# A hybrid decoder trunk on one Trainium2 core: four seven-product pairs in place of three in gate/up groups 1, 4 and 8, and a hold around the first such pair's load

## The chip, the cores and the metric

The program runs on one core of one Trainium2 chip. The core has five engines with an instruction queue each: TensorE (PE, matrix products; its weight loads are listed as PEld), VectorE (DVE), ScalarE (ACT), GpSimd (POOL) and SyncE (SP, which issues the transfers). An engine runs its instructions in the order in which the program holds them. Tiles lie in SBUF; matmul results accumulate in PSUM banks of 128 x 512 float32.

The metric is the device time of one execution in microseconds, the median of several runs. Beside it there is one profiled execution with its trace.

## The reference

Two decoder layers (DEPTH 2) over a residual stream of 256 tokens (SEQ) and 2048 features (D_MODEL), all in float32. The mixers (sliding-window attention with an mLSTM in layer 0, forgetting attention in layer 1) are not touched by the change. What is touched is the feed-forward part, with FFN_HIDDEN = 5632:

```python
def rms_norm(x, g):
    xf = x.astype(jnp.float32)
    y = xf * lax.rsqrt(jnp.mean(xf * xf, axis=-1, keepdims=True) + RMS_EPS)
    return (y * g.astype(jnp.float32)).astype(x.dtype)
...
def swiglu(xn, w_gate, w_up, w_down):
    return (jax.nn.silu(xn @ w_gate) * (xn @ w_up)) @ w_down
...
    for layer in range(DEPTH):
...
        h = h + mix.astype(h.dtype)
        h = h + swiglu(rms_norm(h, norm_ffn[layer]), w_gate[layer], w_up[layer], w_down[layer])
    return rms_norm(h, norm_final)
```

## The kernel before

**Precision.** TensorE multiplies in the format fp32r. To keep float32 accuracy every operand is split into a high part (ACT casts it, L206 or L379) and a low part (DVE subtracts the cast from the value, L207 or L380), and every product is three matmuls: high x high, high x low, low x high (`three`, L556 to L558). So a chunk of weights costs a load, a cast on ACT and a subtraction on DVE before PE can use it.

**Tiling.** The 256 tokens are two row blocks of 128. The contraction over 2048 features is 16 steps of 128, taken as eight pairs of steps. Gate and up are made together in eleven *groups* of 512 columns each; a group multiplies the normalised input (transposed, in `xh` and `xl`) by 512 columns of `w_gate` and 512 of `w_up`, which gives four results of 128 x 512 (two row blocks, gate and up), `acc` in the order. `ffn` runs the groups in three parts (0 to 2, 3 to 6, 7 to 10) and after each part multiplies what it made by the matching rows of `w_down`.

**Two kinds of pairs.** A pair of contraction steps is a 2 x 2 block product: two row blocks by two steps, and two steps by the columns of gate and up. A *plain* pair makes it with 8 products, 24 matmuls: per weight matrix one chunk of 128 x 1024 (`load_chunk`), split by one cast and one subtraction (L206, L207). A *seven-product* pair makes it with 7 products, 21 matmuls, after the scheme of Strassen and Winograd: it loads both chunks into one tile (`quad`), forms three differences of weights on DVE (L646, 128x2x512; L649 and L650, 128x512), and casts and splits three pieces (L379 and L380: one of 128 x 1536 into a triple, two of 128 x 1024 into slots). The matching sums of the inputs are made once per layer ahead of the groups; those for pair 7 (`FOURTH`, with the tile `x4`) are made too. Four of the seven products go into a second set of PSUM banks, `prod`; after the group's last seven-product pair `combine` makes from them one tile `c` of four results (one copy on ACT at L576, three additions on DVE at L578 to L580).

The table `ORDER` sets a group: five plain pairs and three seven-product pairs (1, 3 and 5), two plain ones last. `HEAVY` is a table with four of each, that ends with the plain pair 6. `DENSE` names the groups that use `HEAVY`; it is empty before.

**The end of a group.** Four additions at L697 put the accumulators and `c` together, which also frees their PSUM banks; ACT applies silu; two scaled products at L701 finish; the result goes through two transposing transfers and a `join` that splits it for the down projection. The two sets of PSUM banks change places from group to group (`par`): the `prod` banks of a group are the banks of the previous group's accumulators, so a group's first product waits for an addition at L697.

**Buffers.** Split chunks live in five slots of a high and a low tile (`hi_…`), seven-product pairs in two triples (`hi0_…`/`hi1_…` of 128 x 1536) and three quads; `c` has one buffer.

**What sets the order.** The code is not run in the order in which it is written: a scheduler estimates a timeline for all engines and puts the instructions of each engine in the order of that timeline. So another table of pairs moves instructions on all engines. `tc.issue_after(x)` is a way to hold back what is issued inside its block until x has been placed.

Of the kernel before, what the change touches and what calls it, by code (L numbers as in the profile page):

```python
# [1 line left out]

# [21 lines left out]
NB = 512  # L24
CK = 2
# [10 lines left out]
ORDER = ((0, 0), (1, 1), (0, 2), (1, 3), (0, 4), (1, 5), (0, 6), (0, 7))  # L36
HEAVY = ((1, 1), (0, 0), (1, 3), (0, 2), (1, 5), (0, 4), (1, 7), (0, 6))
FOURTH = 7
DENSE = ()
DOWN = {  # L40
    6: ((0, 0), (1, 1), (0, 2), (1, 3), (0, 4), (0, 5)),
    8: ((0, 0), (1, 1), (0, 2), (1, 3), (0, 4), (1, 5), (0, 6), (0, 7)),
# [33 lines left out]
def trunk(  # L76
# [19 lines left out]
    nc = tc.nc  # L96
# [40 lines left out]
    def load_raw(w, k0, c0, n, pool=wr, bufs=4, raws=None, into=None):  # L137
        if into is not None:
            raw = into
        elif raws:  # L140
            raw = raws.pop(0)
            raws.append(raw)
        else:
            raw = pool.tile([P, CK, NB], F32, tag="raw", name="raw", bufs=bufs)
        loaded[0] = nc.sync.dma_start(
            raw[:, :, 0:n], w[k0 * P : (k0 + CK) * P, c0 : c0 + n].rearrange("(k p) n -> p k n", p=P)
        )
        return raw
# [13 lines left out]
    first = wr.tile([P, CK, NB], F32, tag="raw", name="raw", bufs=4)  # L162
# [96 lines left out]

    sums = {}  # L260

    def square_sum(key, n):
        if n == 0:
            sums[key] = sm.tile([P, NT, 4], F32, tag="ss", name="ss")
        for t in range(NT):
            junk = junk_of[0].tile([P, NB], BF16, tag=junk_of[1], name="junk", bufs=junk_of[2])
            nc.scalar.activation(
                junk, h[:, t, n * NB : (n + 1) * NB], AF.Square, accum_out=sums[key][:, t, n : n + 1]
            )

# [286 lines left out]
        nc.tensor.matmul(o, ah, lo, start=False, stop=False)  # L557
        nc.tensor.matmul(o, al, hi, start=False, stop=stop)  # L558

    def pair_group(fp, par, lhs, sums, mats, order, todo=(), halves=None, inner=None, raws=None):  # L560
        plain = [two_banks(par, "acc") for _ in range(2)]
        begun = set()

# [5 lines left out]
        todo = list(todo)  # L569
# [23 lines left out]
        for pos, (kind, pair) in enumerate(order):  # L593
            k0 = 2 * pair
# [21 lines left out]
            first, last = 1 not in kinds[:pos], 1 not in kinds[pos + 1 :]  # L616
# [5 lines left out]
            if halves:  # L622
                ra, rb = (load_raw(w, k0, c0, NB, fp, W_RAWS, raws) for w, c0 in mats)
                hg, lg = split_chunk(ra, NB)
                run_due(todo, pos)
                hu, lu = (m[:, 0, :] for m in slot())
                split_plain(hu, lu, rb[:, 0, :])
                nc.vector.tensor_tensor(out=ra[:, 1, :], in0=rb[:, 1, :], in1=ra[:, 1, :], op=ALU.subtract)
                nc.vector.tensor_tensor(out=rb[:, 1, :], in0=rb[:, 1, :], in1=rb[:, 0, :], op=ALU.subtract)
                nc.vector.tensor_tensor(out=rb[:, 0, :], in0=rb[:, 0, :], in1=ra[:, 1, :], op=ALU.subtract)  # L630
                nc.vector.tensor_tensor(out=ra[:, 0, :], in0=ra[:, 0, :], in1=rb[:, 0, :], op=ALU.subtract)
                parts = []
                for src in (ra, rb):
                    hs, ls = halves.pop(0)
                    halves.append((hs, ls))
                    split_plain(hs, ls, src)
                    parts += [(hs[:, b, :], ls[:, b, :]) for b in range(CK)]
            else:
                raw = quad()
                for m, (w, c0) in enumerate(mats):  # L640
                    load_raw(w, k0, c0, NB, into=raw[:, CK * m : CK * (m + 1), :])
                hg, lg = triple()
                latest[0] = split_plain(hg, lg, raw[:, 0:3, :])
                hu, lu = hg[:, 2, :], lg[:, 2, :]
                run_due(todo, pos)
                nc.vector.tensor_tensor(  # L646
                    out=raw[:, 1:4:2, :], in0=raw[:, 3:4, :].broadcast_to([P, 2, NB]), in1=raw[:, 1:3, :], op=ALU.subtract
                )
                nc.vector.tensor_tensor(out=raw[:, 2, :], in0=raw[:, 2, :], in1=raw[:, 1, :], op=ALU.subtract)  # L649
                nc.vector.tensor_tensor(out=raw[:, 0, :], in0=raw[:, 0, :], in1=raw[:, 2, :], op=ALU.subtract)  # L650
                (h1, l1), (h0, l0) = slot(), slot()
                split_plain(h1, l1, raw[:, 1:4:2, :])
                split_plain(h0, l0, raw[:, 0:3:2, :])
                parts = [((h0, h1)[b % 2][:, b // 2, :], (l0, l1)[b % 2][:, b // 2, :]) for b in range(4)]
# [14 lines left out]
    def ffn(layer, fp, sx, x4, sd, key, todo, idx_next=None, key_next=None, finish=None):  # L669
# [8 lines left out]
        for g0, g1 in zip(PARTS, PARTS[1:]):  # L678
            end = g1 == PARTS[-1]
            nk = 4 * (g1 - g0)  # L680
            order = DOWN[nk // 2]
            for g in range(g0, g1):
                par = (g1 - 1 - g) % 2
# [5 lines left out]
                    [(w_gate[layer], g * NB), (w_up[layer], g * NB)],  # L689
                    HEAVY if g in DENSE else ORDER,  # L690
                    todo,
                )
                todo = []
                for m in range(2):
# [59 lines left out]
                todo = [(MID if g < g1 - 1 else MID_DOWN, join)]  # L754
# [20 lines left out]
            for n0 in (0, 2):  # L775
# [9 lines left out]
                todo = []  # L785
# [50 lines left out]
    with tc.tile_pool(name="ev", bufs=1) as ev:  # L836
# [225 lines left out]
        with tc.tile_pool(name="mp", bufs=1) as mp:  # L1062
            def sums_m(pair):
# [3 lines left out]
            raws = [  # L1067
                ev.tile([P, CK, NB], F32, tag=tag, name=f"hr{a}", bufs=1 + a // 2)
                for a, tag in enumerate(("kd", "qn", "alibi", "alibi"))
            ]  # L1070
            halves = spare_halves()
# [30 lines left out]
            todo = [(AHEAD_M[m], turn(src, dst)) for m, (src, dst) in enumerate(((qm, qmt), (km, kmt)))]  # L1102
# [92 lines left out]
    with tc.tile_pool(name="od", bufs=1) as od:  # L1195
# [70 lines left out]
        halves = spare_halves()  # L1266
# [152 lines left out]
```

## Time and profile before

| what | value |
|---|---|
| median of 3 runs | 2082.78 us (2081.64 to 2082.93) |
| profiled execution, its own time | 2082.55 us |
| span of its trace | 2080.8 us |
| ACT busy | 1368.0 us |
| POOL busy | 43.2 us |
| 16 DMA engines, mean | 209 GB/s |
| loads of gate and of up | 176 each, 512.0 KB each |

The span runs from the first to the last instruction in the trace. Busy times are per engine; a matmul's shown duration of 0.39 us overlaps the next one, so a stretch of matmuls is measured from start to start. In the trace's rows the columns are the start in us from the span's beginning, the duration in us, the engine, the line, the operation with what it writes and reads (buffer numbers left out) and its size; a bracket behind a row gives the wait ahead of it and what ended it. A row "x2" stands for two instructions on end.

### The profile page before, as it was taken

How to read it: one execution, taken by the hardware profiler on the slowest of the kernel's cores; microseconds unless marked ns; L12 is line 12 of the kernel's file. 1: busy time of each engine (PE TensorE's matmuls, PEld its weight loads, DVE VectorE, ACT ScalarE, POOL GpSimd, SP SyncE). 2: the span in 40 equal slices, each digit the busy share in tenths (PEclk: the TensorE clock that was granted, in tenths of full speed). 3: DMA queues.
4: the chain of work that ended last, by engine and by line, in shares of the span. 5: the costliest groups of instructions: out<-in, count | busy, mean ns of one | idle time of the engine just before them, and what ended most of it. 6: DMA issues, size and time to landing. Idle time of an engine off the chain costs nothing.

```text
span 2080.8 us, 26492 instructions
## 1 busy us (share of the span) xinstructions
PE 2068.0 (99%) x9473; PEld 1715.3 (82%) x9473; DVE 1806.2 (87%) x2169; ACT 1368.0 (66%) x1649; POOL 43.2 (2%) x69
## 2 busy tenths in 40 slices
PE   9999999999999999999999999999999999999998
PEld 8878878888888888888888888887888888888887
DVE  6788768999899989998899688679989999989984
ACT  6777677764576656667676676587655677556763
POOL 1010000000000000000000001000000000000000
PEclk9999999999999999999999999999999999999999
DMA  8566577666676657675676776586756666666754
GB/s 295 175 206 198 188 232 232 225 209 201 191 240 219 205 192 231 210 216 174 201 220 202 227 199 185 182 253 204 229 191 203 224 197 227 219 207 196 238 156 159
DMA packets 309572, 434.84 MB, mean 209 GB/s; under 512 B 106412, under 2 KB 114624, under 8 KB 309312
## 3 DMA queue, kind: packets, MB, share of 16 engines
q1 hardware_dynamic: 307088, 426.27, 65.2%
q0 software_dynamic: 1632, 5.80, 0.9%
q8 instruction: 74, 1.21, 0.2%
q10 hardware_dynamic: 720, 1.09, 0.1%
q14 instruction: 58, 0.48, 0.1%
HBM read 408.68 MB, written 2.12 MB: 197 GB/s over the span
## 4 chain that ended last, share of the span: by engine, by line
PE 87%; DVE 5%; ACT 3%; DMA 2%; issue 2%; SPq 0%; POOL 0%; POOLq 0%; ACTq 0%; DVEq 0%
PE acc L557 20%; PE acc L558 20%; PE acc L556 20%; PE prod L556 5%; PE prod L557 5%; PE prod L558 5%; PE acc L245 4%; PE acc L244 4%; PE acc L246 4%; DVE hi L207 2%; ACT box L345 1%; DMA raw<-in_w_up_dram 1%; PE p L410 1%; DMA raw<-in_w_gate_dram 1%; DMA raw<-in_w_out_even_dram 1%
## 5 line engine op out<-in xcount | busy, mean ns | idle before, releaser
L206 ACT CAST hi<-raw 128x1024 fp32r<-128x1024 f32 (+3 forms) x561 | 567.7, 1023 | 336.9 <-PE acc L558 176.2
L207 DVE TENSOR_TENSOR hi<-raw,hi 128x1024 fp32r<-128x1024 f32 (+3 forms) x561 | 659.8, 1188 | 115.7 <-ACT hi L206 113.8
L558 PE MATMUL acc<-hi,xl 128*128 128x512 f32 x1320 | 512.2, 389 | 0.0
L379 ACT CAST hi<-raw 128x1024 fp32r<-128x1024 f32 (+2 forms) x299 | 345.8, 1169 | 247.3 <-PE acc L558 195.2
L556 PE MATMUL acc<-hi,xh 128*128 128x512 f32 x1320 | 493.6, 390 | 0.1
L557 PE MATMUL acc<-hi,xh 128*128 128x512 f32 x1254 | 488.4, 390 | 1.3 <-DVE hi L207 1.3
L556 PEld LDWEIGHTS acc<-hi,xh 128*128 128x128 f32 x1320 | 247.7, 188 | 51.7 <-ACT hi L206 0.6
L558 PEld LDWEIGHTS acc<-hi,xl 128*128 128x128 f32 x1320 | 247.8, 188 | 51.2
L557 PEld LDWEIGHTS acc<-hi,xh 128*128 128x128 f32 x1254 | 235.4, 188 | 51.9 <-DVE hi L207 2.9
L380 DVE TENSOR_TENSOR hi<-raw,hi 128x1024 fp32r<-128x1024 f32 (+1 forms) x204 | 241.1, 1183 | 18.2 <-ACT hi L379 17.8
L380 DVE TENSOR_TENSOR lo<-raw,hi 128x1536 fp32r<-128x1536 f32 x95 | 166.8, 1756 | 56.1 <-ACT hi L379 55.9
L558 PE MATMUL acc<-hi,ml 128*128 128x512 f32 x466 | 181.0, 389 | 0.0
L556 PE MATMUL acc<-hi,mh 128*128 128x512 f32 x466 | 173.2, 389 | 0.0
L557 PE MATMUL acc<-hi,mh 128*128 128x512 f32 x437 | 170.4, 390 | 0.5 <-DVE hi L207 0.5
L244 PE MATMUL acc<-hi,mh 128*128 128x512 f32 (+1 forms) x322 | 125.2, 391 | 1.4 <-DVE h L394 1.4
L245 PE MATMUL acc<-hi,mh 128*128 128x512 f32 (+1 forms) x322 | 126.3, 392 | 0.0
L246 PE MATMUL acc<-hi,ml 128*128 128x512 f32 (+1 forms) x322 | 123.9, 391 | 0.0
L646 DVE TENSOR_TENSOR raw<-raw 128x1024 f32<-128x1024 f32 x95 | 115.9, 1220 | 0.5
L556 PEld LDWEIGHTS acc<-hi,mh 128*128 128x128 f32 x466 | 87.5, 188 | 18.2
L558 PEld LDWEIGHTS acc<-hi,ml 128*128 128x128 f32 x466 | 87.5, 188 | 18.1
L245 PE MATMUL acc<-hi,xh 128*128 128x512 f32 (+3 forms) x288 | 99.8, 347 | 0.2 <-DVE hi L207 0.2
L246 PE MATMUL acc<-hi,xl 128*128 128x512 f32 (+3 forms) x288 | 99.2, 345 | 0.0
(364 smaller groups left out, 3075.0 us busy)
## 6 DMA issues: line engine op xcount, KB each, us to landing
raw<-in_w_gate_dram SPq DMA_DIRECT2D x176, 512.0 KB, 4.5
raw<-in_w_up_dram SPq DMA_DIRECT2D x176, 512.0 KB, 4.8
raw<-in_w_down_dram SPq DMA_DIRECT2D x176, 512.0 KB, 4.9
raw<-in_w_in_odd_dram SPq DMA_DIRECT2D x88, 512.0 KB, 5.1
raw<-in_w_in_even_dram SPq DMA_DIRECT2D x51, 512.0 KB, 4.8
raw<-in_w_out_even_dram SPq DMA_DIRECT2D x32, 512.0 KB, 5.1
raw<-in_w_out_odd_dram SPq DMA_DIRECT2D x32, 512.0 KB, 5.0
hr<-in_w_in_even_dram SPq DMA_DIRECT2D x12, 512.0 KB, 4.4
```

The source lines that it names most:

```text
L206: latest[0] = nc.scalar.copy(hi[:, k, 0:n], raw[:, k, 0:n])
L207: nc.vector.tensor_tensor(out=lo[:, k, 0:n], in0=raw[:, k, 0:n], in1=hi[:, k, 0:n].bitcast(F32), op=ALU.subtract)
L244: nc.tensor.matmul(o, ah[:, ts], hi, start=(k == 0), stop=False)
L245: nc.tensor.matmul(o, ah[:, ts], lo, start=False, stop=False)
L246: nc.tensor.matmul(o, al[:, ts], hi, start=False, stop=(k == k_all - 1 and cs.stop == n))
L345: nc.scalar.copy(ju[:, :, b], turned[:, b, :, :, :].rearrange("p k t q -> p (k t q)"))
L379: cast = nc.scalar.copy(dst_h, src)
L380: nc.vector.tensor_tensor(out=dst_l, in0=src, in1=dst_h.bitcast(F32), op=ALU.subtract)
L556: nc.tensor.matmul(o, ah, hi, start=start, stop=False)
L557: nc.tensor.matmul(o, ah, lo, start=False, stop=False)
L558: nc.tensor.matmul(o, al, hi, start=False, stop=stop)
L646: nc.vector.tensor_tensor(out=raw[:, 1:4:2, :], in0=raw[:, 3:4, :].broadcast_to([P, 2, NB]), in1=raw[:, 1:3, :], op=ALU.subtract)
```

## The change

It has two parts.

The first is the *hold*. `square_sum` now keeps each of its ACT instructions in a table `marks`; `pair_group` has a new argument `hold`, and group 0 of each layer passes `marks[1]`. The two loads of the group's first seven-product pair are then issued inside `tc.issue_after(hold.ins)`. That call ties only instructions of the engine on which the marked instruction runs, and that is ACT; the block holds nothing but two loads, which SP issues. The rows and the waits of all five engines with this part alone are the same as before it.

The second is `DENSE = (1, 4, 8)`: in these three groups of both layers, six groups in all, `HEAVY` sets the pairs, so that pair 7 becomes a seven-product pair and pair 6 the last, plain one; the seven-product pairs now stand first, third, fifth and seventh.

```diff
-from contextlib import ExitStack
+from contextlib import ExitStack, nullcontext
...
 ORDER = ((0, 0), (1, 1), (0, 2), (1, 3), (0, 4), (1, 5), (0, 6), (0, 7))
 HEAVY = ((1, 1), (0, 0), (1, 3), (0, 2), (1, 5), (0, 4), (1, 7), (0, 6))
 FOURTH = 7
-DENSE = ()
+DENSE = (1, 4, 8)
...
+    marks = {}
+
     def square_sum(key, n):
...
-            nc.scalar.activation(
+            marks[n] = nc.scalar.activation(
                 junk, h[:, t, n * NB : (n + 1) * NB], AF.Square, accum_out=sums[key][:, t, n : n + 1]
             )
...
-    def pair_group(fp, par, lhs, sums, mats, order, todo=(), halves=None, inner=None, raws=None):
+    def pair_group(fp, par, lhs, sums, mats, order, todo=(), halves=None, inner=None, raws=None, hold=None):
...
-                for m, (w, c0) in enumerate(mats):
-                    load_raw(w, k0, c0, NB, into=raw[:, CK * m : CK * (m + 1), :])
+                with tc.issue_after(hold.ins) if hold is not None and first else nullcontext():
+                    for m, (w, c0) in enumerate(mats):
+                        load_raw(w, k0, c0, NB, into=raw[:, CK * m : CK * (m + 1), :])
...
                     HEAVY if g in DENSE else ORDER,
                     todo,
+                    hold=marks[1] if g == 0 else None,
```

The lines behind these move by two to four: L380 becomes L382, L556 to L558 become L558 to L560, L646, L649 and L650 become L649, L652 and L653, L697 becomes L701 and L701 becomes L705. L206 and L207 stay.

In the whole program PE has 18 matmuls fewer, DVE and ACT have 24 and 6 instructions more, and the loads are as many and as large, in another order on SP's queue.

**Layer 0, from group 0 into group 1, on DVE.** Before, from the add that takes group 0's first accumulator (acc_3001 to acc_3004 are its four accumulators, c_3243 its combined tile, raw_2993 to raw_2995 the three quads, hi_2988 to hi_2992 the slots):

```order
L697 TENSOR_TENSOR c_3243<-acc_3001,c_3243 128x512
L649 TENSOR_TENSOR raw_2995<-raw_2995 128x512
L580 TENSOR_TENSOR c_3243<-prod_3038,c_3243 128x2x512
L380 TENSOR_TENSOR hi_2992<-raw_2994,hi_2992 128x1024
L207 TENSOR_TENSOR hi_2988<-raw_3400,hi_2988 128x1024
L650 TENSOR_TENSOR raw_2995<-raw_2995 128x512
L207 TENSOR_TENSOR hi_2989<-raw_3416,hi_2989 128x1024
L697 TENSOR_TENSOR c_3243<-acc_3002,c_3243 128x512
L697 TENSOR_TENSOR c_3243<-acc_3003,c_3243 128x512
L697 TENSOR_TENSOR c_3243<-acc_3004,c_3243 128x512
L380 TENSOR_TENSOR lo1_2987<-raw_2993,hi1_2986 128x1536
L701 TENSOR_SCALAR c_3243<-c_3243,r_2999 128x512
```

And the change, the twelve rows up to the chunk hi_2991<-raw_3448; between the same add at acc_3001 and these stand three more, of 128x512, 128x1024 and 128x2x512:

```order
L382 TENSOR_TENSOR hi_2990<-raw_2994,hi_2990 128x1024
L653 TENSOR_TENSOR raw_2995<-raw_2995 128x512
L382 TENSOR_TENSOR hi_2988<-raw_2995,hi_2988 128x1024
L701 TENSOR_TENSOR c_3243<-acc_3002,c_3243 128x512
L701 TENSOR_TENSOR c_3243<-acc_3003,c_3243 128x512
L701 TENSOR_TENSOR c_3243<-acc_3004,c_3243 128x512
L382 TENSOR_TENSOR lo1_2987<-raw_2993,hi1_2986 128x1536
L705 TENSOR_SCALAR c_3243<-c_3243,r_2999 128x512
L649 TENSOR_TENSOR raw_2993<-raw_2993 128x2x512
L382 TENSOR_TENSOR lo0_2985<-raw_2994,hi0_2984 128x1536
L705 TENSOR_SCALAR c_3243<-c_3243,r_2999 128x512
L207 TENSOR_TENSOR hi_2991<-raw_3448,hi_2991 128x1024
```

The adds at acc_3002 to acc_3004 have one subtraction of 1024 columns fewer ahead of them, and the stretch behind them, up to the chunk that a plain pair of group 1 waits for, now holds another subtraction of 1536 and the difference of 128x2x512 of the next seven-product pair.

**Layer 1, end of group 1 and start of group 2, on PE.** acc_11608 and acc_11609 are accumulators of group 2; hi_10974 holds the chunk raw_11612, hi_10973 the chunk raw_11680, hi0 and hi1 a seven-product pair. Before:

```order
L557 MATMUL acc_11608<-hi_10974,xh_58 128x512
L558 MATMUL acc_11608<-hi_10974,xl_59 128x512
L556 MATMUL acc_11608<-hi0_10968,xh_58 128x512
L557 MATMUL acc_11608<-lo0_10969,xh_58 128x512
L558 MATMUL acc_11608<-hi0_10968,xl_59 128x512
L556 MATMUL acc_11609<-hi_10974,xh_58 128x512
...
L556 MATMUL acc_11609<-hi_10972,xh_58 128x512
L556 MATMUL acc_11608<-hi_10973,xh_58 128x512
```

And the change:

```order
L558 MATMUL acc_11608<-hi_10974,xh_58 128x512
L559 MATMUL acc_11608<-hi_10974,xh_58 128x512
L560 MATMUL acc_11608<-hi_10974,xl_59 128x512
L558 MATMUL acc_11608<-hi1_10970,xh_58 128x512
L559 MATMUL acc_11608<-lo1_10971,xh_58 128x512
L560 MATMUL acc_11608<-hi1_10970,xl_59 128x512
L558 MATMUL acc_11608<-hi_10973,xh_58 128x512
L559 MATMUL acc_11608<-hi_10973,xh_58 128x512
L560 MATMUL acc_11608<-hi_10973,xl_59 128x512
L558 MATMUL acc_11608<-hi_10973,xh_58 128x512
```

Before, acc_11609 takes its turn at hi_10974, and hi_10973 has its first row behind that; with the change acc_11608 goes through hi_10974, the seven-product pair and hi_10973 on end, and the row that reads the low part of hi_10973 stands nine rows behind the one that reads that of hi_10974 (before, 35 rows).

**The same place on DVE.** c_11512 is group 1's combined tile, s4 and sd1 belong to the sums for the down projection, raw_10977 to raw_10979 are the quads. Before, from the one chunk to the other:

```order
L207 TENSOR_TENSOR hi_10974<-raw_11612,hi_10974 128x1024
L646 TENSOR_TENSOR raw_10979<-raw_10979 128x2x512
L578 TENSOR_TENSOR c_11512<-prod_11351,c_11512 128x512
L380 TENSOR_TENSOR sd1_10967<-s4_11525,sd0_10966 128x512
L207 TENSOR_TENSOR hi_10975<-raw_11628,hi_10975 128x1024
L649 TENSOR_TENSOR raw_10979<-raw_10979 128x512
L380 TENSOR_TENSOR hi_10976<-raw_10978,hi_10976 128x1024
L579 TENSOR_TENSOR c_11512<-prod_11350,c_11512 128x512
L697 TENSOR_TENSOR c_11512<-acc_11312,c_11512 128x512
L380 TENSOR_TENSOR hi_10972<-raw_10978,hi_10972 128x1024
L650 TENSOR_TENSOR raw_10979<-raw_10979 128x512
L207 TENSOR_TENSOR hi_10973<-raw_11680,hi_10973 128x1024
```

And the change:

```order
L207 TENSOR_TENSOR hi_10974<-raw_11612,hi_10974 128x1024
L207 TENSOR_TENSOR hi_10975<-raw_11628,hi_10975 128x1024
L653 TENSOR_TENSOR raw_10979<-raw_10979 128x512
L299 TENSOR_TENSOR s4_11520<-c_11227,s4_11520 128x128
L382 TENSOR_TENSOR lo0_10969<-raw_10977,hi0_10968 128x1536
L382 TENSOR_TENSOR hi_10976<-raw_10979,hi_10976 128x1024
L382 TENSOR_TENSOR hi_10972<-raw_10979,hi_10972 128x1024
L649 TENSOR_TENSOR raw_10977<-raw_10977 128x2x512
L207 TENSOR_TENSOR hi_10973<-raw_11680,hi_10973 128x1024
```

The combining adds, the addition at the accumulator and the subtraction for sd1 have moved ahead of the chunk raw_11612; between the two chunks there are now a split of 1536 columns and a difference of 128x2x512 in their place.

## The prediction

> **What bounds the kernel now.** I read the page first, for the engine that is never idle, then windows of the length of one gate/up group, then the timeline for the time between one instruction and the next.
>
> ```profile
> span 2080.8 us, 26492 instructions
> PE 2068.0 (99%) x9473; PEld 1715.3 (82%) x9473; DVE 1806.2 (87%) x2169; ACT 1368.0 (66%) x1649; POOL 43.2 (2%) x69
> PE 87%; DVE 5%; ACT 3%; DMA 2%; issue 2%; SPq 0%; POOL 0%; POOLq 0%; ACTq 0%; DVEq 0%
> ```
>
> PE is busy for 99% and makes 87% of the chain that ended last, so a matmul less is worth its distance to the next one. But DVE's 87% is a mean, and the change works in the gate/up groups alone. Windows of one group each (us; PE, PEld, DVE, ACT, POOL busy with counts; clock; DMA share): layer 0's groups 1, 4, 8, then layer 1's.
>
> ```profile
> 366.30:408.20 41.90, 41.77 (x184) 34.27 (x183) 41.90 (x47) 30.54 (x31) 0.00 (x0) 1.00 0.71 227
> 597.00:639.00 42.00, 42.00 (x187) 34.79 (x186) 40.95 (x46) 29.01 (x30) 0.00 (x0) 1.00 0.70 217
> 883.00:925.00 42.00, 42.00 (x187) 34.75 (x187) 39.76 (x45) 28.15 (x28) 0.00 (x0) 1.00 0.72 215
> 1427.00:1468.00 41.00, 41.00 (x183) 33.95 (x182) 40.47 (x47) 28.96 (x29) 0.00 (x0) 1.00 0.74 237
> 1657.00:1698.00 41.00, 41.00 (x183) 33.96 (x182) 39.94 (x44) 28.14 (x29) 0.00 (x0) 1.00 0.70 222
> 1943.00:1985.00 42.00, 42.00 (x187) 34.80 (x186) 39.76 (x45) 28.16 (x28) 0.00 (x0) 1.00 0.72 218
> ```
>
> In group 1 of layer 0 DVE is busy for 41.90 of 41.90 us, elsewhere for all but 0.5 to 2.2 us. There are two engines at the limit here, and the change takes work from the one and gives it to the other.
>
> **Prices.** PE first: 24 starts lie between these two.
>
> ```profile
> 704.88 0.39 PE L558 MATMUL acc<-hi,ml 128*128 128x512 f32 x1
> 710.32 0.39 PE L558 MATMUL acc<-hi,ml 128*128 128x512 f32 x1
> ```
>
> 5.44 / 24 = 0.2267 us for a matmul (its own 0.39 overlaps the next). DVE back to back, start to start:
>
> ```profile
> 399.09 1.76 DVE L380 TENSOR_TENSOR lo<-raw,hi 128x1536 fp32r<-128x1536 f32 x1
> 400.75 0.29 DVE L297 TENSOR_TENSOR s<-c,s 128x128 f32<-128x128 f32 x1
> 400.96 2.36 DVE L207 TENSOR_TENSOR hi<-raw,hi 128x1024 fp32r<-128x1024 f32 x2
> 403.23 1.22 DVE L646 TENSOR_TENSOR raw<-raw 128x1024 f32<-128x1024 f32 x1
> 404.36 0.69 DVE L578 TENSOR_TENSOR c<-prod,c 128x512 f32<-128x512 f32 x1
> 404.96 0.68 DVE L380 TENSOR_TENSOR sd<-s,sd 128x512 fp32r<-128x512 f32 x1
> 379.45 0.75 DVE L701 SCALAR_TENSOR_TENSOR c<-c,r 128x512 f32<-128x512 f32 x1
> 380.11 1.22 DVE L380 TENSOR_TENSOR hi<-raw,hi 128x1024 fp32r<-128x1024 f32 x1
> ```
>
> So 1536 columns take 1.66, 1024 take 1.135, 512 take 0.60, 128 take 0.21, and the scaled product at L701 takes 0.66.
>
> **The change, part by part.** *The held load* costs nothing: rows and waits are the same with it and without it on all five engines (the part on the change shows why), so there is nothing to hide.
>
> *PE.* A plain pair is 2 x 12 matmuls = 5.44 us, a seven-product pair 7 x 3 = 4.76 us. One pair is exchanged in each of six groups: 18 matmuls fewer, 18 x 0.2267 = **-4.1 us**, all on the path.
>
> *DVE.* A plain pair costs two subtractions of 1024, 2.27 us. A seven-product pair costs one of 1536, three of 1024 and two of 512: 1.66 + 3.40 + 1.20 = 6.27 us. The exchange adds 4.0 us to a group. An old group has 5 x 2.27 + 3 x 6.27, and about 8.6 us outside the pairs (2.34 to combine, 2.4 for four adds, 1.3 for two products, 2.5 for the join): 38.8 us against PE's 183 x 0.2267 = 41.5. A new one has 42.8 against 180 x 0.2267 = 40.8. DVE becomes the longer one by 2.0 us, and must pay from its lead, the time by which it is done before PE needs the result. That the lead, not the mean, decides is seen where the add at L697 frees the bank of a group's first product (layer 0's group 1, layer 1's group 1, layer 0's groups 4 and 8):
>
> ```profile
> 369.65 0.69 DVE L697 TENSOR_TENSOR c<-acc,c 128x512 f32<-128x512 f32 x1
> 371.77 0.39 PE L556 MATMUL prod<-hi,xh 128*128 128x512 f32 x1
> 1427.71 0.68 DVE L697 TENSOR_TENSOR c<-acc,c 128x512 f32<-128x512 f32 x1
> 1431.69 0.39 PE L556 MATMUL prod<-hi,xh 128*128 128x512 f32 x1
> 595.20 0.68 DVE L697 TENSOR_TENSOR c<-acc,c 128x512 f32<-128x512 f32 x1
> 600.84 0.39 PE L556 MATMUL prod<-hi,xh 128*128 128x512 f32 x1
> 884.83 0.69 DVE L697 TENSOR_TENSOR c<-acc,c 128x512 f32<-128x512 f32 x1
> 890.98 0.39 PE L556 MATMUL prod<-hi,xh 128*128 128x512 f32 x1
> ```
>
> The leads are 1.43, 3.30, 4.96 and 5.46 us.
>
> *Layer 0, group 1.* In the new order PE uses that bank 9 matmuls (2.04 us) earlier, DVE frees it 1.14 us earlier (a subtraction of 1024 less ahead of it): the lead there is 1.43 - 2.04 + 1.14 = 0.5 us. From there to the chunk hi_2991<-raw_3448 PE has 56 matmuls, 12.7 us, and DVE the twelve rows shown with the change and three ahead of them, 14.5 us: 0.5 + 12.7 - 14.5 = -1.3. I take **+1.3 us** of new stall. Bounds: 0, if the 1.43 us suffice; 3.3, the whole shortfall of 4.0 + 0.7 less 1.43.
>
> *Layer 1, end of group 1.* Here the new PE order has what the old one has not: it runs the first accumulator of group 2 through three pairs on end, and so asks for the chunk raw_11680 nine matmuls after raw_11612. Before, the same two uses are 7.9 us apart:
>
> ```profile
> 1459.82 2.36 DVE L207 TENSOR_TENSOR hi<-raw,hi 128x1024 fp32r<-128x1024 f32 x2
> 1467.50 0.39 PE L557 MATMUL acc<-hi,xh 128*128 128x512 f32 x1
> 1475.43 0.39 PE L557 MATMUL acc<-hi,xh 128*128 128x512 f32 x1
> ```
>
> Between the two chunks DVE has five of 1024 (the last one included), one of 1536, one of 512 and one of 128: 8.1 us; PE has nine matmuls, 2.04. The lead at the first is 5.3 us before (1467.50 less the end of the pair of subtractions that begins at 1459.82). The new order takes from it 0.7 (fewer matmuls ahead), 1.5 (DVE rows moved ahead) and 1.0 (waits that PE no longer makes, next) and leaves 2.1. So 2.1 + 2.0 - 8.1 = -4.0, **+4.0 us**. Bounds by the same rows: the lead kept whole gives 0.8, none left gives 6.1.
>
> *Waits that fall away.* Both are in layer 1's first group:
>
> ```profile
> 1414.96 0.50 PE L557 MATMUL acc<-hi,xh 128*128 128x512 f32 x1 [0.32 <-DVE hi L207]
> 1426.11 0.50 PE L557 MATMUL acc<-hi,xh 128*128 128x512 f32 x1 [0.67 <-DVE hi L207]
> ```
>
> In the new order these chunks are used some matmuls later; 0.32 + 0.67 gives **-1.0 us** (0 if they only move).
>
> *Groups 4 and 8, and the pairs behind them.* Added up row by row, the lead in the new order falls by at most some 3 to 4 us below its value at the group's start, 4.96 or 5.46, and the combining adds now wait for products that end one plain pair before the group's end, not two. What is left is between 0.8 and 2 us: no stall in the sum of rows, but little room. I take **+0.8 us** for all four groups and the way into the down projections; bounds 0 and 2.0 per group.
>
> *ACT and DMA.* ACT casts one 1536 more per new group:
>
> ```profile
> L379 ACT CAST hi<-raw 128x1536 fp32r<-128x1536 f32 x95 | 140.8, 1483 | 68.0 <-PE acc L558 31.3 <-PE prod L558 24.8 <-DMA raw<-in_w_up_dram 6.8
> raw<-in_w_gate_dram SPq DMA_DIRECT2D x176, 512.0 KB, 4.5
> ```
>
> 1.5 us on an engine that is busy for 28 to 31 of 42 us. The loads are as many and as large; on SP's queue they only change places. Both nothing, covered by ACT's idle time; if ACT's cast stood ahead of a late subtraction it would be 1.5 us a group, within the bound above.
>
> *The clock.* PE's longest pause before is 1.8 us, and it does not lower the clock:
>
> ```profile
> 278.31 0.39 PE L246 MATMUL acc<-hi,ml 128*128 128x512 f32 x1
> 280.14 0.50 PE L244 MATMUL acc<-hi,mh 128*128 128x512 f32 x1 [1.44 <-DVE h L394]
> 276.00:282.00 6.00, 4.56 (x20) 3.44 (x20) 5.50 (x6) 4.21 (x7) 0.00 (x0) 1.00 0.69 259
> ```
>
> The Trainium skill, "TensorE: Matmul & The Clock Gate" (HAM oscillation), speaks against a single long pause: an idle stretch over some 3.4 us halves TensorE's clock until it has been busy for such a stretch again. The pause that I expect in layer 1 is of that size; an estimate by that page's figure would be 1.7 us more, 2085.5 in all. No row here shows a pause so long, and I leave it out of the sum.
>
> **Sum.** -4.1 + 1.3 + 4.0 - 1.0 + 0.8 = +1.0 us. The profiled execution took 2082.55 us (span 2080.8), the median of the runs is 2082.78: 2083.6 by the one, **2083.8 us** by the other, which I predict. What PE saves, it loses again waiting for DVE. 0.2%, 4.2 us, is about what a measurement of this kernel can tell from no change.
>
> **Rivals.** (1) *Slower: DVE is the bound in every new group.* If the lead at groups 4 and 8 does not carry, each pays its 2.0 us, and the group behind, which begins with DVE late, about as much again: 4 x 2.0 to 4 x 3.5 more, so 2091 to 2097. For it: 42.8 us against 40.8, and ACT casts that DVE waits for stand in one queue with casts that wait for PE. Against: leads of 5 us, and DVE idle for 1.1 to 2.2 us in those windows. It decides once the lead at a group's start is below 3 us. (2) *Faster: the lead covers all.* Then 4.1 and the 1.0 count in full, 2077.7. For it: before, PE waits only twice for long in these groups. Against: the 8.1 us of DVE work against 2.04 of PE. (3) *The held load does hold*, and the first pair of each layer comes late or early: no row shows it; it would move one load of 4.5 us and end within 0.2%.
>
> **Numbers.** My forecast, with the cases of 2079 to 2087, 0.62; rival 1 0.26, rival 2 0.11, rival 3 0.01, which counts with the first. The sum's own bounds: all low, -4.1 + 0 + 0.8 - 1.0 = -4.3, 2078.5; all high, -4.1 + 3.3 + 6.1 + 8 = +13.3, 2096. Eight times in ten I expect 2078.5 to 2091.0: from the low bound to the first price of rival 1. Faster by over 0.2% 0.11, within 0.63, slower 0.26.
>
> **What would show it.** PE has 18 matmuls fewer at the same 0.227 us. DVE's busy time grows by some 24 us (6 x 4.0). Windows of the six groups show DVE at 100%. A PE pause of 3 to 4 us behind layer 1's group 1, released by DVE's subtraction at the line that is L207 now, and pauses of 1 to 2 us in layer 0's group 1. No pause over 1 us in groups 4, 5, 8 and 9: if there are such, rival 1 is right. If the pause in layer 1 is missing, my sum of DVE's rows is wrong there, and the time is near 2080.

## The result and the profile after

The changed kernel takes 2095.02 us (median of 6 runs, 2093.03 to 2097.52); before, 2082.93 us (6 runs, 2081.64 to 2083.21). The ratio is 1.0058, 95% interval 1.0048 to 1.0068: 12.1 us slower. The forecast was 2083.8 us and its range ended at 2091.0.

The page of the changed kernel, in the lines that answer to those shown of before:

```profile
span 2091.9 us, 26353 instructions
PE 2070.1 (99%) x9455; PEld 1710.4 (82%) x9455; DVE 1826.7 (87%) x2193; ACT 1369.7 (65%) x1655; POOL 44.2 (2%) x69
PE 75%; DVE 11%; DMA 5%; ACT 5%; issue 4%; SPq 1%; POOL 0%; ACTq 0%; POOLq 0%; DVEq 0%
```

PE has its 18 matmuls fewer, and still 99%, which says little here: pauses of 0.2 to 2.6 us that make the span 11 us longer are half a per cent of it. The chain of waits says more. PE made 87% of it and makes 75% now; DVE has gone from 5% to 11%, DMA from 2% to 5%.

To see where the time went, I took from both traces the start of the last matmul of each group's accumulators, and the time from one such point to the next (us):

| stretch | before | after | difference |
|---|---|---|---|
| start to the end of layer 0's group 0 | 365.88 | 366.59 | +0.7 |
| layer 0: groups 1, 2 and the first unit of the down projection | 116.19 | 120.81 | **+4.6** |
| layer 0: second unit, groups 3 to 6 | 196.97 | 197.63 | +0.7 |
| layer 0: next down projection, groups 7 to 10 | 248.88 | 248.20 | -0.7 |
| layer 0: last down projection | 83.91 | 85.55 | **+1.6** |
| layer 1's mixer and group 0 | 413.00 | 412.93 | -0.1 |
| layer 1: groups 1, 2 and the first unit | 116.92 | 120.41 | **+3.5** |
| layer 1: second unit, groups 3 to 6 | 196.98 | 198.36 | **+1.4** |
| layer 1: the rest | 334.06 | 333.38 | -0.7 |

The sum is 11.0, the difference of the spans 11.1. The three matmuls that each dense group saves, 0.7 us, are in these differences; the stretches of group 8 keep them, those of groups 1 and 4 lose more than they save. A few matmuls also change sides at a boundary with the new order: counted in the traces, layer 0's stretch with group 1 holds 5 fewer (1.1 us) and layer 1's 6 fewer (1.4 us), and the stretches ahead of them hold 2 and 3 more. (A "unit" is a pair of column blocks of the down projection.)

Layer 1's group 1 first. On PE, the first accumulator of group 2 waits:

```profile
1474.79 0.50 PE L558 MATMUL acc<-hi,xh 128*128 128x512 f32 x1 [2.18 <-ACT c L578]
```

It needs a PSUM bank that held product 0 of group 1, until ACT copies it into `c` (L578). ACT, in the same stretch:

```profile
1468.11 2.43 ACT L381 CAST hi<-raw 128x1536 fp32r<-128x1536 f32 x2 [0.35 <-DMA raw<-in_w_up_dram]
1471.54 1.05 ACT L381 CAST hi<-raw 128x1024 fp32r<-128x1024 f32 x1 [0.99 <-DVE raw L653]
1472.69 1.04 ACT L206 CAST hi<-raw 128x1024 fp32r<-128x1024 f32 x1
1473.64 0.61 ACT L381 CAST sd<-s 128x512 fp32r<-128x512 f32 x1
1474.16 0.58 ACT L578 COPY c<-prod 128x512 f32<-128x512 f32 x1
```

And DVE:

```profile
1467.32 3.50 DVE L207 TENSOR_TENSOR hi<-raw,hi 128x1024 fp32r<-128x1024 f32 x3
1470.72 0.70 DVE L653 TENSOR_TENSOR raw<-raw 128x512 f32<-128x512 f32 x1
1471.33 0.30 DVE L299 TENSOR_TENSOR s<-c,s 128x128 f32<-128x128 f32 x1
1471.53 1.77 DVE L382 TENSOR_TENSOR lo<-raw,hi 128x1536 fp32r<-128x1536 f32 x1
```

The copy is a job of 0.58 us, but it is late: on ACT it stands behind a cast that waits 0.99 us for DVE's difference at L653, and behind two more casts. Nor could it have come before 1471.63: `c` has one buffer, and DVE's last reading of group 0's `c` (the sum at L299) ends only then, behind a queue of splits without a gap. So a busy DVE reaches PE through an ACT row. The new order adds to it, because the group's last products now come one plain pair before its end and not two. Before, the same copy ended at 1460.58, 6.7 us ahead of the start of the group's last matmul (1467.27), and PE went on without a pause:

```profile
1459.99 0.59 ACT L576 COPY c<-prod 128x512 f32<-128x512 f32 x1 [0.35 <-DVE s L297]
```

The pause has a second price. Windows around it, of the changed kernel (us; PE, PEld, DVE, ACT, POOL busy; clock; DMA share; GB/s):

```profile
1470.00:1472.20 2.20, 2.20 (x11) 1.84 (x10) 2.20 (x4) 1.21 (x2) 0.00 (x0) 1.00 1.05 386
1475.00:1476.00 1.00, 1.00 (x5) 0.82 (x5) 1.00 (x2) 0.00 (x0) 0.00 (x0) 1.00 0.14 49
1476.00:1477.00 1.00, 1.00 (x4) 0.74 (x4) 1.00 (x2) 0.00 (x0) 0.00 (x0) 0.50 0.44 29
1478.00:1479.00 1.00, 1.00 (x4) 0.85 (x3) 1.00 (x3) 0.00 (x0) 0.00 (x0) 0.50 0.88 313
1482.00:1484.00 2.00, 2.00 (x10) 1.66 (x9) 1.97 (x4) 1.72 (x2) 0.00 (x0) 1.00 0.04 8
```

The clock is halved from 1476.0 to 1479.4. Seven matmuls start 0.427 us apart instead of 0.227: 1.4 us more.

In layer 0 the delay surfaces later. Group 1 and group 2 lose 0.5 and 1.0 us, the first unit of the down projection 3.1. PE there:

```profile
459.92 0.50 PE L559 MATMUL acc<-hi,mh 128*128 128x512 f32 x1 [0.81 <-DVE hi L207]
472.05 0.50 PE L558 MATMUL acc<-hi,mh 128*128 128x512 f32 x1 [0.71 <-ACT mh L381]
475.11 0.50 PE L558 MATMUL acc<-hi,mh 128*128 128x512 f32 x1 [0.46 <-ACT hi L381]
```

ACT ahead of that waits for loads, and DVE for ACT:

```profile
445.22 1.05 ACT L206 CAST hi<-raw 128x1024 fp32r<-128x1024 f32 x1 [2.02 <-DMA raw<-in_w_down_dram]
447.91 1.48 ACT L381 CAST hi<-raw 128x1536 fp32r<-128x1536 f32 x1 [1.64 <-DMA raw<-in_w_down_dram]
```

```profile
446.31 1.23 DVE L207 TENSOR_TENSOR hi<-raw,hi 128x1024 fp32r<-128x1024 f32 x1 [0.85 <-ACT hi L206]
449.43 1.76 DVE L382 TENSOR_TENSOR lo<-raw,hi 128x1536 fp32r<-128x1536 f32 x1 [1.90 <-ACT hi L381]
```

The loads of the down weights are issued on SP's queue behind the transposing transfers of group 1's result. In the two timelines of that queue (SP; the x4 row is the four transfers of one group):

```profile
425.02 5.12 SPq L732 DMA_TRANSPOSE turned<-c  x4
430.24 0.53 SPq L145 DMA_DIRECT2D raw<-in_w_up_dram  x1
430.81 16.75 SPq L145 DMA_DIRECT2D raw<-in_w_down_dram  x10
```

```profile
432.65 5.12 SPq L736 DMA_TRANSPOSE turned<-c  x4
437.87 0.53 SPq L145 DMA_DIRECT2D raw<-in_w_up_dram  x1
438.44 9.49 SPq L145 DMA_DIRECT2D raw<-in_w_down_dram  x9
```

The upper one is before, the lower one after: the transposes start 7.6 us later, because the additions and products that finish group 1 are late on DVE, and the loads behind them on the queue are late by as much. The last of these products, before and after:

```profile
421.17 0.75 DVE L701 SCALAR_TENSOR_TENSOR c<-c,r 128x512 f32<-128x512 f32 x1
430.74 0.75 DVE L705 SCALAR_TENSOR_TENSOR c<-c,r 128x512 f32<-128x512 f32 x1
```

The second and third of PE's three waits (0.71 and 0.46 us) have another source. ACT casts `mh`, here the transposed result of group 2. Before, that cast stands between two casts of 1536 columns; after, both of these stand ahead of it:

```profile
465.82 1.07 ACT L379 CAST mh<-pf 128x512 fp32r<-128x512 f32 x2
467.25 1.50 ACT L379 CAST hi<-raw 128x1536 fp32r<-128x1536 f32 x1
```

```profile
468.66 2.85 ACT L381 CAST hi<-raw 128x1536 fp32r<-128x1536 f32 x2 [0.50 <-PE prod L560]
471.42 1.07 ACT L381 CAST mh<-pf 128x512 fp32r<-128x512 f32 x2
```

What differs here is the order that the scheduler gave ACT. The same two waits, of the same length, stand in layer 1's first unit.

### The profile page after: what moved, and what is told of

Its sections match the earlier page's. It is cut to its first block, busy times and chain, and to the rows that moved or that the text cites. A ratio compares the mean times of both kernels' runs of the same rounds, so it can differ in the third digit from the quotient of the medians.

```text
span 2091.9 us, 26353 instructions
## 1 busy us (share of the span) xinstructions
PE 2070.1 (99%) x9455; PEld 1710.4 (82%) x9455; DVE 1826.7 (87%) x2193; ACT 1369.7 (65%) x1655; POOL 44.2 (2%) x69
## 3 DMA queue, kind: packets, MB, share of 16 engines
q8 instruction: 74, 1.21, 0.2%
## 4 chain that ended last, share of the span: by engine, by line
PE 75%; DVE 11%; DMA 5%; ACT 5%; issue 4%; SPq 1%; POOL 0%; ACTq 0%; POOLq 0%; DVEq 0%
PE acc L559 17%; PE acc L560 16%; PE acc L558 16%; PE prod L559 4%; PE prod L558 4%; PE prod L560 4%; PE acc L245 3%; PE acc L244 3%; DVE hi L207 3%; PE acc L246 3%; DVE hi L382 1%; DMA raw<-in_w_up_dram 1%; DMA raw<-in_w_down_dram 1%; ACT hi L206 1%; ACT box L347 1%
## 5 line engine op out<-in xcount | busy, mean ns | idle before, releaser
L206 ACT CAST hi<-raw 128x1024 fp32r<-128x1024 f32 (+2 forms) x549 | 555.0, 1022 | 356.1 <-PE acc L560 181.7
L207 DVE TENSOR_TENSOR hi<-raw,hi 128x1024 fp32r<-128x1024 f32 (+2 forms) x549 | 648.1, 1189 | 131.8 <-ACT hi L206 129.6
L381 ACT CAST hi<-raw 128x1024 fp32r<-128x1024 f32 (+2 forms) x317 | 364.5, 1169 | 213.6 <-PE acc L560 92.7
L560 PE MATMUL acc<-hi,xl 128*128 128x512 f32 x1284 | 499.0, 390 | 0.0
L558 PE MATMUL acc<-hi,xh 128*128 128x512 f32 x1284 | 476.7, 391 | 3.0 <-ACT c L578 2.2
L559 PE MATMUL acc<-hi,xh 128*128 128x512 f32 x1212 | 472.0, 390 | 0.8 <-DVE hi L207 0.7
L558 PEld LDWEIGHTS acc<-hi,xh 128*128 128x128 f32 x1284 | 241.2, 188 | 55.2 <-ACT c L578 2.6
L560 PEld LDWEIGHTS acc<-hi,xl 128*128 128x128 f32 x1284 | 241.3, 188 | 50.1
L382 DVE TENSOR_TENSOR hi<-raw,hi 128x1024 fp32r<-128x1024 f32 (+1 forms) x216 | 255.7, 1188 | 15.9 <-ACT hi L381 15.8
L559 PEld LDWEIGHTS acc<-hi,xh 128*128 128x128 f32 x1212 | 227.7, 188 | 49.7 <-DVE hi L207 2.5
L382 DVE TENSOR_TENSOR lo<-raw,hi 128x1536 fp32r<-128x1536 f32 x101 | 177.3, 1757 | 39.2 <-ACT hi L381 39.1
L560 PE MATMUL acc<-hi,ml 128*128 128x512 f32 x466 | 179.0, 389 | 0.0
L558 PE MATMUL acc<-hi,mh 128*128 128x512 f32 x466 | 171.8, 390 | 2.4 <-ACT mh L381 1.4
L649 DVE TENSOR_TENSOR raw<-raw 128x1024 f32<-128x1024 f32 x101 | 123.4, 1222 | 0.2
L558 PEld LDWEIGHTS acc<-hi,mh 128*128 128x128 f32 x466 | 87.5, 188 | 22.1 <-ACT mh L381 1.9
L560 PEld LDWEIGHTS acc<-hi,ml 128*128 128x128 f32 x466 | 87.5, 188 | 18.0
```

The costliest lines, as they stand in the source:

```text
L206: latest[0] = nc.scalar.copy(hi[:, k, 0:n], raw[:, k, 0:n])
L207: nc.vector.tensor_tensor(out=lo[:, k, 0:n], in0=raw[:, k, 0:n], in1=hi[:, k, 0:n].bitcast(F32), op=ALU.subtract)
L381: cast = nc.scalar.copy(dst_h, src)
L382: nc.vector.tensor_tensor(out=dst_l, in0=src, in1=dst_h.bitcast(F32), op=ALU.subtract)
L558: nc.tensor.matmul(o, ah, hi, start=start, stop=False)
L649: nc.vector.tensor_tensor(out=raw[:, 1:4:2, :], in0=raw[:, 3:4, :].broadcast_to([P, 2, NB]), in1=raw[:, 1:3, :], op=ALU.subtract)
```

## The experiments

Beside each group of four kernels the kernel before was run on the same chip; "+x" is the difference of the medians, and behind it stands the ratio, estimated from the runs by itself, with its interval. All edits are against the changed kernel unless said otherwise.

### Which part of the change it is

The hold alone:

```diff
-DENSE = (1, 4, 8)
+DENSE = ()
```

> The hold alone, DENSE empty. Theory A (the rows of the changed order: the hold ties nothing on the engine that issues the loads, all of the +12.1 us comes from the dense groups): 2082.9, within 1 us of before, and no pause of PE over 0.5 us that before does not have. Rival H (the held loads come late and start the delay): several us above before, with the delay beginning in group 0.

Measured: 2084.13 against 2084.07, ratio 0.9998 (0.9989 to 1.0007). The hold costs nothing; rival H falls.

One dense group at a time, `DENSE = (1,)`, `(4,)` and `(8,)`:

> Only group 1 of each layer dense, hold kept. Between the ends of the units of four accumulators, the changed kernel is late by 5.2 us over layer 0's groups 0 to 2 and the first down projection behind them, and by 3.6 us over the same stretch of layer 1. Theory A (each dense group pays on its own, in the stretch up to the next down projection): +8.8 us, about 2091.7. Rival B (DVE is the bound in every dense group alike, so the three groups share the +12.1 equally): +4, about 2087.

> Only group 4 dense. Theory A, from the same table (0.7 us over layer 0's groups 3 to 6, 1.4 us over layer 1's): +2.0, about 2085, with one pause of PE in group 5 of each layer, where ACT waits for the load of a seven-product pair. Rival B: +4, about 2087.

> Only group 8 dense. Theory A: three matmul pairs, 6 matmuls, come off and nothing is lost, because DVE's lead at its first product is 7.4 us there: -1.4 us, about 2081.5; if the pause of 1.4 us at the end of layer 0's last down projection belongs to it as well, +0.2, about 2083. Rival B: +4, about 2087.

Measured: group 1 +7.8 (1.0037; 1.0025 to 1.0050), group 4 +1.2 (1.0005; 0.9996 to 1.0015), group 8 +0.9 (1.0001; 0.9992 to 1.0011). Group 1 is two thirds of the change's cost, and an equal price for all three (rival B) falls. The three add up to 9.9 of 12.1 us; the intervals leave room for the rest. The table of stretches puts the pauses where the full change has them: group 1 alone lengthens its stretch by 3.7 us in layer 0 and by 3.5 in layer 1; group 4 alone lengthens groups 3 to 6 by 0.6 and 0.7 us, its own saving taken off; group 8 gains 0.7 in each layer and loses 1.0 in layer 0's last down projection. For groups 4 and 8 these small figures are single profiles; the runs alone don't tell them from nothing. (Whole spans of single profiles compare worse than stretches: near 280 us, in the mixer, each has a pause that no edit touches, of 1.57 to 2.80 us.)

The lead of 7.4 us that two of the expectations give for group 8 is a misreading: it takes the instruction queue's semaphore at 801.10 for the addition. The addition starts at 802.71 (rows below, in the part on groups 4 and 8), and the lead is 5.7 us.

### Is it DVE's work, or the order of the pairs?

Four kernels with group 1 alone. First the old order with DVE work added and no matmul removed (against before; `more` is set in group 1):

```diff
+            if again[0]:
+                nc.vector.tensor_tensor(
+                    out=lo[:, k, 0:n], in0=raw[:, k, 0:n], in1=hi[:, k, 0:n].bitcast(F32), op=ALU.subtract
+                )
...
+                    again[0] = more and pair == 4
                     hi, lo = load_chunk(w, k0, c0, NB)
...
                 latest[0] = split_plain(hg, lg, raw[:, 0:3, :])
+                if more and pair == 3:
+                    nc.vector.tensor_tensor(out=lg, in0=raw[:, 0:3, :], in1=hg.bitcast(F32), op=ALU.subtract)
```

> The old order of pairs in all groups; in group 1 of each layer three subtractions are made twice (one of 1536 columns, two of 1024), which adds 1.66 + 2 x 1.135 = 3.9 us of DVE work a group, as much as a fourth seven-product pair adds, and takes no matmul away. Theory D (what is paid in group 1 is DVE's added work): the pauses of the kernel with group 1 dense come again, without the 1.4 us that it saves: +7 to +9 us against before. Theory P (what is paid is the place of the last products: the combining adds have one plain pair, 5.4 us, until PE needs the product banks, where before they had two): within 1 us of before.

Measured: +6.6 (1.0028; 1.0017 to 1.0040). DVE work by itself, in the old order of pairs, makes most of the pauses: 6.6 us, where group 1 dense has 9.2 (7.8 and the 1.4 us of matmuls that it saves). Theory P falls as the main cause.

The three differences of the fourth seven-product pair left out (L649 to L653, DVE):

```diff
+                if pair != FOURTH:
-                nc.vector.tensor_tensor(
+                    nc.vector.tensor_tensor(
...
```

> Only group 1 dense, and in its fourth seven-product pair the three differences of weights are left out, so that the exchange adds 1.7 us of DVE work a group instead of 4.0; matmuls, casts and loads stay. Theory D: less than half of the delay stays, +1 to +4 us against before. Theory P: it stays at +6 to +8.

Measured: +5.4 (1.0026; 1.0015 to 1.0036), between the two theories: 4.7 us less DVE work in the two layers took 2.4 us off the 7.8.

The same seven-product pairs with two plain pairs last:

```diff
-HEAVY = ((1, 1), (0, 0), (1, 3), (0, 2), (1, 5), (0, 4), (1, 7), (0, 6))
+HEAVY = ((1, 1), (0, 0), (1, 3), (0, 2), (1, 5), (1, 7), (0, 4), (0, 6))
```

> Only group 1 dense, with the same four seven-product pairs, but the two plain pairs 4 and 6 last, so that the last products end two plain pairs before the group's end, as before the change. Theory D: as with the order of the change, +6 to +9 us. Theory P: the pause of 2.6 us behind layer 1's group 1 and the late additions in layer 0 fall away: -1 to +2 us.

Measured: +13.4 (1.0065; 1.0050 to 1.0080), worse than with the order of the change and outside both forecasts. It puts two seven-product pairs in succession, and the delay sits in group 2 (47.8 us instead of 41.5 in layer 0, 48.0 in layer 1). In layer 1 the clock is halved there for 6.83 us, behind a pause of 3.90 us from start to start. Moving the last products forward doesn't help when it packs DVE's work closer; what their place alone costs, this run does not show.

The differences on GpSimd:

```diff
+                eng = nc.gpsimd if pair == FOURTH else nc.vector
-                nc.vector.tensor_tensor(
+                eng.tensor_tensor(
...
```

> Only group 1 dense, and the three differences of its fourth seven-product pair run on GpSimd, which is idle there, in place of DVE. Theory D: as without the differences if GpSimd is about as fast as DVE, +1 to +4 us; if it takes several times DVE's 1.1 us for 1024 columns the casts behind it come late and the gain is lost. Theory P: +6 to +8.

Measured: +11.5 (1.0056; 1.0041 to 1.0071), above both forecasts. GpSimd's group of these rows, and what it did in layer 0's group 1:

```profile
L650 POOL TENSOR_TENSOR raw<-raw 128x1024 f32<-128x1024 f32 x2 | 9.6, 4797 | 100.5 <-DVE lo L382 100.5
```

```profile
382.92 2.84 POOL L650 TENSOR_TENSOR raw<-raw 128x1024 f32<-128x1024 f32 x1 [50.77 <-DVE lo L382]
385.84 2.14 POOL L653 TENSOR_TENSOR raw<-raw 128x512 f32<-128x512 f32 x1
388.05 1.60 POOL L654 TENSOR_TENSOR raw<-raw 128x512 f32<-128x512 f32 x1
```

```profile
383.42 3.42 DVE L207 TENSOR_TENSOR hi<-raw,hi 128x1024 fp32r<-128x1024 f32 x1
386.76 1.76 DVE L653 TENSOR_TENSOR raw<-raw 128x512 f32<-128x512 f32 x1
391.80 1.21 DVE L207 TENSOR_TENSOR hi<-raw,hi 128x1024 fp32r<-128x1024 f32 x1
```

GpSimd takes 2.84 and 6.76 us, 4.8 in the mean, for what DVE does in 1.2, and a DVE subtraction that meets it takes 3.42 us instead of 1.21. The work taken off DVE comes back as waiting inside DVE's own rows. So this run decides nothing between D and P.

Then two pairs' differences left out, so that group 1 has no more DVE work than an old one (the edit against the kernel above that leaves out the fourth pair's):

```diff
-                if pair != FOURTH:
+                if pair != FOURTH and not (order is HEAVY and pair == 5):
```

> Only group 1 dense, and the three differences of weights are left out in two of its four seven-product pairs, so that the group has 0.7 us less DVE work than an old one (4.0 - 2 x 2.34). Theory D (DVE's work alone sets the delay): nothing is left of it and the 6 matmuls count, -1.4 us, at most +1 against before. Theory O (the new order of the pairs costs something by itself; one exchange without differences still cost +5.4 with 1.7 us of added work a group): +2 to +4.

Measured: +1.5 (1.0009; 1.0000 to 1.0018), between theory D (at most +1) and theory O (+2 to +4). Most of the delay has gone with the work, but the 1.4 us of matmuls are not gained. The stretch from group 1 to the first unit of the down projection, layer 0 and layer 1, in windows as above. Before:

```profile
365.90:482.10 116.20, 115.87 (x514) 95.23 (x513) 110.99 (x123) 76.59 (x78) 0.00 (x0) 1.00 0.64 209
1424.80:1541.80 117.00, 116.03 (x514) 95.22 (x513) 110.27 (x121) 75.02 (x76) 0.00 (x0) 1.00 0.64 208
```

After:

```profile
366.60:487.40 120.80, 117.51 (x509) 93.42 (x507) 114.96 (x127) 77.18 (x78) 0.00 (x0) 1.00 0.63 201
1431.70:1552.10 120.40, 116.74 (x507) 94.95 (x506) 114.03 (x125) 75.24 (x76) 0.00 (x0) 0.99 0.63 201
```

Subtractions made twice, in the old order:

```profile
366.30:486.50 120.20, 117.50 (x513) 94.48 (x512) 115.76 (x127) 76.33 (x78) 0.00 (x0) 1.00 0.65 202
1430.40:1549.60 119.20, 116.65 (x513) 94.77 (x512) 114.55 (x126) 74.94 (x76) 0.00 (x0) 1.00 0.64 204
```

Differences left out in two of four pairs:

```profile
367.60:484.80 117.20, 115.65 (x509) 93.90 (x508) 110.26 (x121) 76.71 (x78) 0.00 (x0) 1.00 0.63 207
1426.90:1544.10 117.20, 115.07 (x508) 93.84 (x507) 108.94 (x118) 75.66 (x77) 0.00 (x0) 1.00 0.66 207
```

Read the first and the fourth number after the window: its length, and DVE's busy time. Before, DVE is busy for 111.0 of 116.2 us and idle for 5.2; after, 115.0 of 120.8, idle for 5.8. With the subtractions made twice it is 115.8 of 120.2. DVE's idle time of 4 to 8 us in this stretch does not give way (it waits there for loads and for ACT, as in the rows above), so what is added to DVE lengthens the stretch. Between the last kernel and the change, over both layers, DVE's work differs by 9.8 us and the time by 6.8. What is left is not the amount of DVE's work: with 2.1 us less of it and 11 matmuls (2.5 us) fewer in them than before, six of them saved and five moved ahead, the two stretches are still 1.2 us longer. So of the 10.5 us of new pauses in them (8.0 net and 2.5), about 6.8 go with DVE's work and 3.7 do not.

The traces show where the 3.7 sit. In the last kernel's layer 0 the transposes of group 1's result start at 422.56, earlier than before, so the late loads did go with DVE's work; but PE's two waits for ACT's casts in the first unit are still there, with 0.70 and 0.45 us. In its layer 1 PE waits 1.62 us in the first unit for the copy of product 0 (ACT, L578). The two waits for casts stand in the kernel with subtractions made twice too, where the order of pairs is the old one, and not in the last kernel's layer 1. So they belong to the scheduler's order on ACT, which every one of these edits can move, and the split into 6.8 and 3.7 is no clean one. No kernel here holds ACT's order fixed while DVE's work changes; that stays open.

### Is there a group that can take it?

`DENSE = (3, 7)`, `(0, 3, 7)` and `(3, 7, 8)`:

> Groups 3 and 7 dense, the first of their parts, in place of 1, 4 and 8. Before the change DVE is busy for 37.5 of 41.3 us in group 3 and 37.3 of 41.5 in group 7, where it is 41.9 of 41.9 in group 1. Theory D (an exchange is free where DVE's idle time in the stretch covers its 4.0 us): 4 x 3 matmuls fewer, -2.7 us. Rival R (DVE's idle time there is waiting for loads and slots, which does not give way): each group pays about 2 us, +4 to +6.

> Groups 0, 3 and 7 dense. Before the change DVE is idle for 8.1 of 41.6 us in group 0. Theory D: 18 matmuls fewer and no new pause, -4.1 us. Rival R: group 0's idle time is waiting for the layer's start (loads, the input's sums) and group 1 behind it has none to give, so group 1's pauses come again: +4 to +8.

> Groups 3, 7 and 8 dense, two in succession. Theory D: group 8 alone saved 0.7 us in each layer and cost 1.0 us at the end of layer 0's last down projection, so about -3 us, if DVE's lead of 7.4 us at group 8 carries both. Rival R: the second of two dense groups in succession finds the lead spent, and group 9 pays 2 to 4 us in each layer: +2 to +6.

Measured: +1.9 (1.0009; 1.0000 to 1.0018), +17.8 (1.0084; 1.0070 to 1.0097) and +3.9 (1.0020; 1.0011 to 1.0029). The first lies between the two forecasts, the second far above both, the third in rival R's range. By the profiles, group 7 keeps its 0.7 us in both layers, as group 8 does; group 3 pays some 1.5 us of pauses in each layer (a part of them in group 5) and so loses 0.8; group 7 and 8 in succession lose 0.2 instead of gaining 1.4, with a pause of 1.5 us in group 8. Group 0 takes 50.7 us instead of 41.6 in layer 0 and 51.5 instead of 41.9 in layer 1: early in it DVE waits for ACT (2.51 us in layer 0) and ACT for a load (2.36 us), as rival R had it; later DVE works without a gap while PE pauses 3.03 us from start to start for it, and the clock is halved for 6.83 us in each layer, which R did not have. That a stretch shows DVE idle does not make it room. No kernel here beats the one before. Group 7 alone, or group 8 in layer 1 alone, might save about a microsecond by these profiles, less than the runs can tell; neither was run.

## Why the prediction was wrong

Of the terms of the sum, -4.1 came as forecast and -1.0 nearly so. The other three, +1.3, +4.0 and +0.8, came as some 5.7, 4.9 and 5.0 us of added pauses in their stretches.

*The hold* was right: +0.1 us, and no new pause in the stretches.

*PE's part* was right: 18 matmuls fewer at 0.227 us, -4.1 us, seen undisturbed in group 8.

*DVE's price* was nearly right: 24 us more busy time forecast, 20.5 measured (1806.2 to 1826.7).

*The balance of a group* is the step that failed first. "An old group has ... 38.8 us against PE's 183 x 0.2267 = 41.5" was a sum over one group's own rows. The window quoted beside it said that DVE was busy for 41.90 of 41.90 us in layer 0's group 1. A window over group 2, which I did not take then, has 40.4 of 41.5, with joins, sums and the next unit's splits among the rows (before; DVE is the fourth number behind the window):

```profile
407.80:449.30 41.50, 41.50 (x185) 34.37 (x184) 40.44 (x45) 28.88 (x29) 0.00 (x0) 1.00 0.67 217
```

DVE's idle time behind group 1 was 1.1 us and not 2.7, and the idle time that I saw elsewhere was waiting.

*Layer 0, group 1*, "+1.3 us of new stall", was mis-sized. I followed the lead to one chunk in group 1 and closed the account there. The lateness was carried on through the end of group 1, the transposes on SP's queue and the loads behind them, into the first unit of the down projection. The stretch is 4.6 us longer with 5 matmuls (1.1 us) fewer in it: 5.7 us of new pauses, outside the bound of 3.3. Of these, 1.2 us are the two waits for ACT's casts, which no term of the sum had.

*Layer 1, end of group 1*, "+4.0 us", came at its place and near its size: group 2 took 45.8 us instead of 41.5. The row was another. Not the chunk raw_11680 held PE, but the copy of product 0 at L578, late behind the same DVE queue; 1.4 of the 4.3 us is the halved clock. I had left the clock out because no row showed a pause as long as the one that I expected. The clock fell after a pause of 2.57 us between two starts. The Trainium skill ("TensorE: Matmul & The Clock Gate", HAM oscillation) puts the limit at an idle stretch over some 3.4 us. Here the measurement decides; a pause shorter than that figure is not safe. The first unit of the down projection added 1.1 us that I had no term for, the same two waits for ACT's casts.

*The waits that fall away*, -1.0, were right: the pauses in layer 1's groups 0 and 1, the long one behind group 1 left out, went from 1.8 to 0.9 us (the length of the stretch less 0.2267 us for each matmul in it).

*Groups 4 and 8*, "+0.8 us", was wrong, and for a plain reason: the windows and leads that I gave for groups 4 and 8 are those of groups 5 and 10. I had counted the groups by their additions, and came out one too far for group 4 and two for group 8. Group 4 begins at 554.8 and group 8 at 803.7. The rows that belong there, additions and first products of group 4 and of group 8, before:

```profile
553.78 0.68 DVE L697 TENSOR_TENSOR c<-acc,c 128x512 f32<-128x512 f32 x1
558.68 0.39 PE L556 MATMUL prod<-hi,xh 128*128 128x512 f32 x1
802.71 1.28 DVE L697 TENSOR_TENSOR c<-acc,c 128x512 f32<-128x512 f32 x2
809.15 0.39 PE L556 MATMUL prod<-hi,xh 128*128 128x512 f32 x1
```

The leads are 4.2 and 5.7 us, not far from those that I used, so it was not this that made the number wrong. What did was the point at which I looked. Group 4 itself paid nothing; group 5 paid, when ACT waited for a seven-product pair's load whose quad DVE had freed late (rows of ACT and PE, after):

```profile
617.44 2.44 ACT L381 CAST hi<-raw 128x1536 fp32r<-128x1536 f32 x2 [5.49 <-DMA raw<-in_w_up_dram]
622.51 0.50 PE L559 MATMUL prod<-hi,sx 128*128 128x512 f32 x1 [0.99 <-DVE hi L382]
```

Pauses of 1.3 us in layer 0 and 2.1 in layer 1 behind group 4, and 1.6 us in layer 0's last down projection behind group 8, make 5.0 us where I had 0.8. I had called the loads free because they are as many and as large. They are; but they are issued when DVE frees a tile, and a late split becomes a late load of 5 to 6 us. ACT's extra cast I had called covered by its idle time; what PE then waited for were ACT rows that came late in ACT's order, the copy at L578 and the cast of `mh`.

*The rivals.* The time came out in the range that rival 1 gave, 2091 to 2097, to which I gave 0.26, but not as it described: it had groups 4 and 8 paying 2.0 to 3.5 us each, the group behind included, while two thirds of the cost is group 1's. Rival 2 failed, rival 3 too.

## What to carry to other kernels

Before an exchange of one engine's work for another's, read the receiving engine's busy time in the very stretch, over its neighbours too, and ask what its idle time waits for: idle time that is waiting is no room. Follow lateness to the end of the chain (the finish of the tile, the transfers queued behind it, the loads that start when a tile is freed) and not to the first wait where it fits. And name a window's stage from the instructions in it, not by counting.

## What the runs showed of the hardware

TensorE's granted clock fell to 0.50 for 3.41 us after a pause of 2.57 us between two matmul starts, about 1.2 us after the matmuls had begun again; before, a pause of 1.83 us left it at 1.00. The length of a pause does not decide it alone: in the mixer, pauses of 2.60 us (group 8 dense), 2.63 us (the hold alone) and 2.80 us (groups 0, 3 and 7) left the clock at 1.00, and one of 2.64 us (groups 3, 7 and 8) halved it for 3.41 us. What else decides was not settled.

GpSimd's elementwise work slows DVE: a subtraction of 128x1024 took 3.42 us beside a GpSimd difference and 1.21 us without. The Trainium skill has that under "SBUF — State Buffer", Who interferes with whom (a DVE instruction with two SBUF inputs contends with a GpSimd instruction that reads SBUF), and the trace agrees: 3.42 against 1.21 us.
